# Hybrid attention layer on one core: q and k transposed in full by head pairs and split behind the transpose, first column sums ahead of the root's turn, two modulations together

## The chip, the core and the metric

One core of a Trainium2 chip runs the whole layer as one program. Its engines are TensorE (PE, with PEld for the weight loads that overlap its matmuls), VectorE (DVE), ScalarE (ACT), GpSimd (POOL) and SyncE (SP, which here issues most DMAs). The metric is the device time of one execution in microseconds.

## The reference

In outline. One decoder layer on a sequence of 512 tokens of width 1024. x is normalised by its root mean square and modulated by a scale and a shift computed from c; the result h goes through one wide projection to q, k, v and gates of two groups of eight heads of width 64, two key heads each.

```python
mod = silu(c) @ w_ada + b_ada
shift, scale, gate = split(mod, 3)
h = rms_norm(x, norm_gain) * (1 + scale) + shift
(q_a, k_a, v_a, z_a, q_b, kc, vc, ks, vs, kw, vw, z_b, g_b) = split(h @ w_in)
qa = qk_norm(q_a) * qscale;  ka = qk_norm(k_a)          # group A: window 128, sinks
o_a = banded_gqa(qa, ka, v_a, 128, rel_bias_a, sinks)
qb = qk_norm(q_b) * qscale                               # group B: three branches
k_cmp = qk_norm(compress(kc)); k_sel = qk_norm(ks); k_win = qk_norm(kw)
o_b = g0 * compressed(qb) + g1 * selected(qb) + g2 * window_512(qb)
y = concat(o_a * silu(z_a), o_b * silu(z_b))
out = x + gate * (y @ w_out)
```

With 8 blocks of 64 keys and a top-k of 16 the selected branch takes all blocks, so it is causal attention too.

## The kernel before

The sequence lies in four blocks of 128 tokens (NB = 4), the width in eight tiles of 128 (k = 0 to 7). A product that must keep f32 accuracy is made of three products in the faster type fp32r: each operand is split into a high part (a copy rounded to fp32r, on ACT) and a low part (the difference, on DVE), and high x high, high x low and low x high are summed in PSUM.

**First projection** (lines 300 to 438, in a strict written order on every engine, `in_order`). The squares of x are summed by matmuls, `rsqrt` is made on DVE from four columns, and `rbp` is its transposed broadcast, four PE transposes (L369), "the root's turn". For each width tile k the modulation needs two vectors: `mod_pe(k)` makes partial sums on PE (L228, evicted by ACT at L232 to `macc`), or `mod_dve(k)` makes them on DVE; `mod_col(k)` sums them over the partitions by PE (L259); `mod_ab(k)` (L264, L265) makes scale and shift from them, and `h_high` and `h_low` the two parts of h. `first_proj(k, n)` is PE's work for tile k and product n. `MOD_AFTER` says after which (k, n) which `mod_pe` stands, `COL_AFTER` the same for `mod_col`. Weights come through rings of NR = 4 slots, which SP's loads refill when a slot is read.

**The rest** is a list of slots, run four deep in a software pipeline (`run`): scores of a slot (L892) with their maximum on DVE (L897), exponentials on ACT, scaling, transposes of the probabilities (L940, L950, evicted by ACT at L941, L951), products with v (L967). Between the parts of a slot a `Stream` of other work, a generator, is advanced by a number of microseconds: every `yield` names the cost of the PE work just issued. The stream holds the other projections (`unit_nat` L484, `unit_col` L494, with weights split at L170 on ACT and L171 on DVE) and, one step of a "post" to one step of a unit, the preparation of q, k, gates and compressed keys. Outside the blocks of PE work that are ordered by hand, the tile framework plans the order of instructions on each engine at build.

**q and k.** `q_scale` is called for a pair of heads, four times for group A and four for group B; `k_scale` once for each of three key sets. Both normalise on DVE (`qn` L532, `kn` L555 and L557), split into high and low parts in `qc` or `kc` (ACT L535 or L559, DVE L536 or L560), and transpose the parts on PE with an fp32r identity (L541, L565) into two PSUM banks one after the other, four transposes each. For q a bank holds one head, high part in partitions 0 to 63 and low part in 64 to 127, evicted in one piece with reversed order in each block (`qs`, ACT L549 or DVE L547). For k a bank holds the high (then the low) parts of both key heads, and each is evicted twice, into both halves of the partitions (`kT`, ACT L569, DVE L570). `PT` gives out the two PSUM banks of all transposes in turn. The scores multiply 128 rows of `qs` (high and low) with `kT[:, 0]` (high twice) and `kT[:, 1]` (low twice).

The **last projection** (L494 with `yh`, `yl`) makes eight output tiles, each evicted by DVE with gate and residual (L1048) and stored.

Of the kernel before, what the change touches and what calls it, by code (L numbers as in the profile page):

```python
# [9 lines left out]
F32 = mybir.dt.float32  # L10
F32R = mybir.dt.float32r
I32 = mybir.dt.int32
BF16 = mybir.dt.bfloat16
AF = mybir.ActivationFunctionType
OP = mybir.AluOpType
# [4 lines left out]
S, D, HD, NB = 512, 1024, 64, 4  # L20
# [5 lines left out]
LINE = 640  # L26
GW = 280
AHEAD = 6
NT2 = 38
WAIT_L, WAIT_M = 4, (0, 8)  # L30
PER_A, PER_B = 3.6, (3.5, 1.6, 7)
ND = (16, 3, 4)
NR = 4
LW = 4
MOD_AFTER = {(0, 0): (1,), (1, 0): (2,), (2, 0): (3,), (3, 2): (5,)}
COL_AFTER = {(0, 1): (1,), (1, 1): (2,), (2, 1): (3,), (3, 1): (4,), (4, 0): (5,), (5, 0): (6,), (6, 1): (7,)}


def rev(ap):

    dims = [list(e) for e in ap.ap]
    step, n = dims[-1]
    dims[-1] = [-step, n]
    return bass.AP(tensor=ap.tensor, offset=ap.offset + step * (n - 1), ap=dims)
# [37 lines left out]
def hybrid_layer_kernel(ctx, tc, A, out):  # L82
    nc = tc.nc
    PE, DVE, ACT, POOL, SP = nc.tensor, nc.vector, nc.scalar, nc.gpsimd, nc.sync
# [3 lines left out]
    con = ctx.enter_context(tc.tile_pool(name="con", bufs=1))  # L88
    t2 = ctx.enter_context(tc.tile_pool(name="t2", bufs=NT2))
    rawp = ctx.enter_context(tc.tile_pool(name="rawp", bufs=5))  # L90
# [3 lines left out]
    def T2(dt, name):  # L94
        return t2.tile([128, S], dt, name=name, tag="t2")
# [17 lines left out]
    cT, prm, ident = first[:, 0:8], first[:, 8:40], first[:, 40:168]  # L113
# [4 lines left out]
    cmask = rest[:, 832:960].rearrange("p (a b) -> p a b", a=NB)  # L118
    qga, kga, qgb, kgs, kgw, kgc = (sml[:, 64 * i:64 * i + 64] for i in range(6))
    bnsa, sinks = sml[:, 384:408], sml[:, 408:416]  # L120
    ident_r = con.tile([128, 128], F32R, name="ident_r")
    ones = con.tile([128, 1], F32, name="ones")
    DVE.memset(ones, 1.0)

# [98 lines left out]
    def mod_pe(k):  # L223

        pm = ps_pj.tile([128, 512], F32, name="pj")[:, 0:256]
        for j in range(8):
            c = j % 4
            PE.matmul(pm[32 * c:32 * c + 32, :], scz[:, j, :], ada[k][:, j].rearrange("p a b -> p (a b)"),  # L228
                      start=j < 4, stop=j >= 4, skip_group_check=True)
        macc[k] = stp.tile([128, 2, 128], F32, name="macc0", bufs=2)  # L230
        yield
        ACT.activation(macc[k].rearrange("p a b -> p (a b)"), pm, AF.Copy)  # L232
# [22 lines left out]
    def mod_col(k):  # L255

        pc = pcs[k] = ps_pj.tile([128, 512], F32, name="pj")
        for s in range(2):
            PE.matmul(pc[:, s:s + 1], macc[k][:, s, :], ones, start=True, stop=True)  # L259
# [8 lines left out]
    def weights_high(k):  # L268

        ws[k] = (stp.tile([128, 768], F32R, name="swh", bufs=3), stp.tile([128, 768], F32R, name="swl", bufs=3))  # L270
        ACT.activation(ws[k][0], wst[k], AF.Copy)
# [4 lines left out]
    def scaled(k, by, parts=(slice(0, S),)):  # L276
        y[k] = xT[k]
        for c in parts:
            DVE.tensor_tensor(y[k][:, c], xT[k][:, c], by[:, c], op=OP.mult)
# [19 lines left out]
    with in_order(tc) as begun:  # L299
# [20 lines left out]
        def dummies(n):  # L320
            for _ in range(n):
                PE.matmul(pj_kv[0].rearrange("p a b -> p (a b)"), zero[:, 0:128], zero, start=True, stop=True)
# [3 lines left out]
        halves = [slice(0, 256), slice(256, 512)]  # L326
# [29 lines left out]
                              stop=k == 7 and tb == NB - 1, skip_group_check=True)  # L356
        for b in lines[2:]:
            next(b, None)
        ACT.activation(ident_r, ident, AF.Copy)
        for a in range(2):  # L360
            SP.dma_start(line_d[a], lsb[a])
        sx = con.tile([128, NB], F32, name="sx")
# [1 line left out]
        rx = rsqrt(sx, NB)  # L364
        for _ in mod_pe(0):
            pass
        rbp = ps_pj.tile([128, 512], F32, name="pj")
        for tb in range(NB):
            PE.transpose(rbp[:, tb * 128:(tb + 1) * 128], rx[:, tb:tb + 1].to_broadcast([128, 128]), ident)  # L369
        mod_col(0)  # L370
        dummies(ND[2])
        weights_high(0)
        scaled(0, rbp, halves[:1])
        mod_ab(0)
        scaled(0, rbp, halves[1:])
        rb = stp.tile([128, S], F32, name="rb")
        hf[0] = T2(F32, "hf")
        for c in halves:
# [36 lines left out]
        for k in range(8):  # L415
# [6 lines left out]
            for n in range(3):  # L422
                first_proj(k, n)
                for m in MOD_AFTER.get((k, n), ()):
                    for _ in mod_pe(m):
# [14 lines left out]
    mp = ctx.enter_context(tc.tile_pool(name="mp", bufs=1))  # L440

    def W2(name, shape=(128, 512)):
        return mp.tile(list(shape), F32, name=name, tag="w2", bufs=5)
# [22 lines left out]
    def PT():  # L466
        return ps_t.tile([128, 512], F32, name="pt")
# [36 lines left out]
        chain.update(last)  # L504


    qs = {}
    kT = {}
    kTb = {}
# [18 lines left out]

    def q_scale(src, rn, heads):

        qn = W2("qn", (128, 8, HD))
        DVE.tensor_tensor(qn.rearrange("p (t h) d -> p t h d", t=NB), src,  # L532
                          rn[:, :, :, None].to_broadcast([128, NB, 2, HD]), op=OP.mult)
        qc = mp.tile([128, 8, 2, HD], F32R, name="qc", tag="qc", bufs=2)
        ACT.activation(qc[:, :, 0, :], qn, AF.Copy)  # L535
        DVE.tensor_tensor(qc[:, :, 1, :], qn, qc[:, :, 0, :].bitcast(F32), op=OP.subtract)  # L536
        yield 0.0
        for n, h in enumerate(heads):
            pt = PT()
            for tb in range(NB):  # L540
                PE.transpose(pt[:, tb * 128:(tb + 1) * 128].bitcast(F32R),  # L541
                             qc[:, 2 * tb + n].rearrange("p a d -> p (a d)"), ident_r)
            qs[h] = T2(F32R, f"qs{h}")
            dst = qs[h].rearrange("p (t q) -> p t q", t=NB)
            src_ = rev(pt.rearrange("p (t q) -> p t q", t=NB))
            if n:
                DVE.tensor_copy(dst, src_)  # L547
            else:
                ACT.activation(dst, src_, AF.Copy)  # L549
            yield 0.44  # L550

    def k_scale(ty, src, rn):

        kn = W2("kn", (128, 8, HD))
        DVE.tensor_tensor(kn, src.rearrange("p t (g d) -> p (t g) d", d=HD), rn[:, :, None].to_broadcast([128, 8, HD]),  # L555
                          op=OP.mult)
        DVE.tensor_tensor(kn, kn, kg[:, ty:ty + 1, :].to_broadcast([128, 8, HD]), op=OP.mult)  # L557
        kc = mp.tile([128, 2, 8, HD], F32R, name="kc", tag="qc", bufs=2)
        ACT.activation(kc[:, 0], kn, AF.Copy)  # L559
        DVE.tensor_tensor(kc[:, 1], kn, kc[:, 0].bitcast(F32), op=OP.subtract)  # L560
        yield 0.0
        for hl_ in range(2):
            pt = PT()
            for t in range(NB):
                PE.transpose(pt[:, t * 128:(t + 1) * 128].bitcast(F32R),  # L565
                             kc[:, hl_, 2 * t:2 * t + 2].rearrange("p g d -> p (g d)"), ident_r)
            for g in range(2):
                src_ = pt[64 * g:64 * g + 64, :]
                ACT.activation(kT[ty, g][0:64, hl_, :], src_, AF.Copy)  # L569
                DVE.tensor_copy(kT[ty, g][64:128, hl_, :], src_)  # L570
            yield 0.44

    rn_a = {}

# [545 lines left out]
```

## Time and profile before

| | |
|---|---|
| median of 3 runs | 325.29 us (324.1 to 432.5) |
| profiled execution, its own time | 324.27 us |
| its span from the first to the last instruction | 322.2 us |
| PE, PEld, DVE, ACT busy | 97%, 80%, 73%, 61% |
| granted TensorE clock | 0.999 of full |

Busy time of PE includes the latency of matmuls that overlap, so a busy PE isn't PE at its peak. Times in the trace are counted from the first instruction of the span. PE is the same engine as PEld; a wait can show on either of the two queues or on both.

### The profile page before, as it was taken

To read this page: it belongs to the slowest core of one execution; us is meant where nothing else is said; L and a number is where in the kernel's file an instruction comes from. 1 tells how busy PE (TensorE), PEld (TensorE's weight loads), DVE (VectorE), ACT (ScalarE), POOL (GpSimd) and SP (SyncE) were. 2 spreads that over 40 slices of the span, in tenths; PEclk is the share of its full clock that TensorE was granted. 3 is DMA by queue.
4 is the path that set the end of the run, shared out by engine and by line. 5 is a ranking of instruction groups with operands and counts; after the bars stand their busy time and mean duration, and the time that the engine had idled before them with its cause. 6 is when DMAs were issued, how large, how long until landed. Compare 5 with 4: busy or idle time off the path is not lost.

```text
span 322.2 us, 6131 instructions
## 1 busy us (share of the span) xinstructions
PE 312.7 (97%) x2232; PEld 259.0 (80%) x2232; DVE 235.6 (73%) x691; ACT 196.2 (61%) x477; POOL 4.9 (2%) x22
## 2 busy tenths in 40 slices
PE   7899999999999999999999999999999999999995
PEld 2577888888999888989977787788788788788883
DVE  3658597999888268878899789899779788544320
ACT  4565545965986474986958658787587575502200
POOL 1000000000010000000000000000000000000000
PEclk9999999999999999999999999999999999999999
DMA  8999975800065248130042270045422134034301
GB/s 238 394 409 409 400 240 133 301 3 3 0 189 172 67 137 290 34 113 21 33 130 41 94 197 0 2 125 203 131 67 70 63 110 152 33 101 166 125 33 65
DMA packets 31061, 44.26 MB, mean 137 GB/s; under 512 B 1767, under 2 KB 23399, under 8 KB 31033
## 3 DMA queue, kind: packets, MB, share of 16 engines
q1 hardware_dynamic: 29880, 41.79, 38.8%
q10 hardware_dynamic: 1152, 2.10, 2.4%
q8 instruction: 17, 0.28, 0.3%
q14 instruction: 12, 0.09, 0.1%
HBM read 41.74 MB, written 2.14 MB: 136 GB/s over the span
## 4 chain that ended last, share of the span: by engine, by line
PE 73%; DVE 14%; DMA 6%; ACT 4%; issue 2%; SPq 1%; DVEq 0%; ACTq 0%
PE pj L494 23%; PE pj L484 9%; PE sq L295 7%; PE s L892 6%; PE po L967 6%; PE skv L296 4%; PE pt L940 3%; DMA raw<-in_w_z_b 3%; PE pt L950 3%; DVE wl L171 3%; DVE pp L897 2%; PE s L620 2%; PE pj L228 2%; DMA raw<-in_bias 1%; DMA raw<-in_w_q_b 1%
## 5 line engine op out<-in xcount | busy, mean ns | idle before, releaser
L170 ACT ACTIVATE wh<-raw 128x512 fp32r<-128x512 f32 (+1 forms) x52 | 31.2, 635 | 25.0 <-PE pj L494 14.6
L171 DVE TENSOR_TENSOR wl<-raw,wh 128x512 fp32r<-128x512 f32 (+1 forms) x52 | 35.2, 691 | 8.1 <-ACT wh L170 4.6
L484 PE MATMUL pj<-wh,hh 128*128 128x256 f32 (+1 forms) x128 | 36.8, 289 | 0.4 <-ACT wh L170 0.4
L484 PE MATMUL pj<-wh,hl 128*128 128x256 f32 (+1 forms) x128 | 36.9, 288 | 0.0
L484 PE MATMUL pj<-wl,hh 128*128 128x256 f32 (+1 forms) x128 | 36.4, 286 | 0.0
L904 ACT ACTIVATE pp<-pp,nm 128x256 f32<-128x256 f32 (+2 forms) x48 | 29.3, 612 | 5.9 <-DVE nm L897 5.4
L494 PE MATMUL pj<-hh,wh 128*128 128x512 f32 x80 | 32.6, 407 | 0.0
L494 PE MATMUL pj<-hh,wl 128*128 128x512 f32 x80 | 32.1, 402 | 0.0
L494 PE MATMUL pj<-hl,wh 128*128 128x512 f32 x80 | 31.9, 399 | 0.0
L897 DVE CUSTOM_DVE_ANT_0 pp<-s,bias 128x256 f32<-128x256 f32 (+2 forms) x48 | 25.6, 548 | 4.6 <-PE s L892 4.6
L494 PE MATMUL pj<-yh,wl 128*128 128x512 f32 x64 | 25.5, 398 | 0.0
L494 PE MATMUL pj<-yh,wh 128*128 128x512 f32 x64 | 25.4, 399 | 0.0
L494 PE MATMUL pj<-yl,wh 128*128 128x512 f32 x64 | 25.3, 395 | 0.0
L484 PEld LDWEIGHTS pj<-wh,hh 128*128 128x128 f32 x128 | 24.0, 188 | 0.6 <-ACT wh L170 0.6
L484 PEld LDWEIGHTS pj<-wl,hh 128*128 128x128 f32 x128 | 24.1, 189 | 0.2 <-issue 0.2
L484 PEld LDWEIGHTS pj<-wh,hl 128*128 128x128 f32 x128 | 24.1, 188 | 0.1
L892 PE MATMUL s<-kTb,qs 128*128 128x256 f32 (+2 forms) x96 | 23.4, 357 | 0.0
L897 DVE CUSTOM_DVE_ANT_0 pa<-s,bias,nsink 128x256 f32<-128x256 f32 (+1 forms) x32 | 14.3, 448 | 10.5 <-PE s L892 9.1
L951 ACT COPY ptT<-pt 128x384 f32<-128x384 f32 (+1 forms) x32 | 16.0, 527 | 9.3 <-PE pt L950 8.5
L925 DVE TENSOR_SCALAR pp<-pp,rr,grev 128x256 f32<-128x256 f32 (+2 forms) x48 | 21.4, 473 | 0.3
L1048 DVE SCALAR_TENSOR_TENSOR fin<-pj,gate,xr 128x512 f32<-128x512 f32 x8 | 6.0, 751 | 20.1 <-PE pj L494 20.1
L941 ACT COPY ptT<-pt 128x512 f32<-128x512 f32 (+1 forms) x28 | 15.4, 549 | 7.7 <-PE pt L940 7.4
(240 smaller groups left out, 727.6 us busy)
## 6 DMA issues: line engine op xcount, KB each, us to landing
ada_ring<-in_w_ada_ss SPq DMA_DIRECT2D x16, 512.0 KB, 7.3
raw<-in_w_cmp SPq DMA_DIRECT2D x8, 512.0 KB, 7.6
raw<-in_w_gate SPq DMA_DIRECT2D x8, 512.0 KB, 4.7
raw<-in_w_o SPq DMA_DIRECT2D x8, 512.0 KB, 3.8
wst_ring<-in_w_qkv_a SPq DMA_DIRECT2D x8, 384.0 KB, 9.3
xTp<-in_xT SPq DMA_DIRECT2D x8, 256.0 KB, 4.5
bias<-line_d SPq DMA_DIRECT2D x8, 256.0 KB, 3.8
raw<-in_w_q_b SPq DMA_DIRECT2D x4, 512.0 KB, 4.3
```

What stands on the lines that cost most here:

```text
L170: ACT.activation(wh, src, AF.Copy)
L171: DVE.tensor_tensor(wl, src, wh.bitcast(F32), op=OP.subtract)
L295: PE.matmul(pj_q[tb], lt, w[:, 0:512], start=f, stop=l, skip_group_check=True)
L484: PE.matmul(bank[:, t * n:(t + 1) * n], h[:, tb * 128:(tb + 1) * 128], w[:, k % 2, :], start=k == 0 and m == 0, stop=k == 7 and m == 2)
L494: PE.matmul(bank, w, h, start=k == 0 and m == 0, stop=k == 7 and m == 2)
L892: PE.matmul(ps, qs[h][:, 128 * i:128 * i + 128], k[:, hl_, lo:lo + w], start=hl_ == 0, stop=hl_ == 1)
L897: DVE.tensor_tensor_reduce(out=P[:, g, 0:w], in0=ps, in1=bt, scale=1.0, scalar=init, op0=OP.add, op1=OP.min, accum_out=nm[:, g:g + 1])
L904: ACT.activation(P[:, g, 0:e], P[:, g, 0:e], AF.Exp, bias=nm[:, g:g + 1], scale=-1.0, accum_out=dn[:, g:g + 1])
L925: DVE.tensor_scalar(v, v, rr[:, g:g + 1], gates[:, g, br:br + 1], op0=OP.mult, op1=OP.mult)
L941: ACT.copy(T[:, :, 0:nb, :], rev(pt[:, 0:2 * nb * 128].rearrange("p (g b q) -> p g b q", g=2, b=nb)))
L951: ACT.copy(T[:, 0:nb, :], rev(pt[:, 0:nb * 128].rearrange("p (b q) -> p b q", b=nb)))
L967: PE.matmul(o[64 * g:64 * g + 64, 128 * i:128 * i + 128], vb[:, 64 * g:64 * g + 64], sl["T"][g][:, b, :], start=first_of and b == 0, stop= ...
```

## The change

Four edits. (1) `q_scale` and `k_scale` transpose the normalised f32 values of a pair of heads at once, four transposes into one bank with the f32 identity, and make the two parts while evicting: ACT writes the rounded high part, DVE subtracts it from the same half of the bank. For the second head of a pair the high part lies in partitions 64 to 127 and the low one in 0 to 63. The tiles `qc`, `kc` and the fp32r identity `ident_r` go, each generator has one `yield 0.44` less, and the ring of general tiles has 40 slots instead of 38 (`NT2`). (2) `mod_col(0)` stands ahead of the four transposes of the root instead of behind them. (3) `mod_ab(0)` stands ahead of both halves of `scaled(0)` on DVE instead of between them. (4) `mod_pe(3)` stands right behind `mod_pe(2)`, after product 0 of tile 1, instead of after product 0 of tile 2.

```diff
-NT2 = 38
+NT2 = 40
...
-MOD_AFTER = {(0, 0): (1,), (1, 0): (2,), (2, 0): (3,), (3, 2): (5,)}
+MOD_AFTER = {(0, 0): (1,), (1, 0): (2, 3), (3, 2): (5,)}
...
-    ident_r = con.tile([128, 128], F32R, name="ident_r")
...
-        ACT.activation(ident_r, ident, AF.Copy)
...
         for _ in mod_pe(0):
             pass
+        mod_col(0)
         rbp = ps_pj.tile([128, 512], F32, name="pj")
         for tb in range(NB):
             PE.transpose(rbp[:, tb * 128:(tb + 1) * 128], rx[:, tb:tb + 1].to_broadcast([128, 128]), ident)
-        mod_col(0)
         dummies(ND[2])
         weights_high(0)
-        scaled(0, rbp, halves[:1])
         mod_ab(0)
-        scaled(0, rbp, halves[1:])
+        scaled(0, rbp, halves)
...
+    HALF = (slice(0, 64), slice(64, 128))
...
     def q_scale(src, rn, heads):
         qn = W2("qn", (128, 8, HD))
         DVE.tensor_tensor(qn.rearrange("p (t h) d -> p t h d", t=NB), src,
                           rn[:, :, :, None].to_broadcast([128, NB, 2, HD]), op=OP.mult)
-        qc = mp.tile([128, 8, 2, HD], F32R, name="qc", tag="qc", bufs=2)
-        ACT.activation(qc[:, :, 0, :], qn, AF.Copy)
-        DVE.tensor_tensor(qc[:, :, 1, :], qn, qc[:, :, 0, :].bitcast(F32), op=OP.subtract)
         yield 0.0
+        pt = PT()
+        for tb in range(NB):
+            PE.transpose(pt[:, tb * 128:(tb + 1) * 128], qn[:, 2 * tb:2 * tb + 2].rearrange("p a d -> p (a d)"), ident)
+        blocks = lambda ap: ap.rearrange("p (t q) -> p t q", t=NB)
         for n, h in enumerate(heads):
-            pt = PT()
-            for tb in range(NB):
-                PE.transpose(pt[:, tb * 128:(tb + 1) * 128].bitcast(F32R),
-                             qc[:, 2 * tb + n].rearrange("p a d -> p (a d)"), ident_r)
             qs[h] = T2(F32R, f"qs{h}")
-            dst = qs[h].rearrange("p (t q) -> p t q", t=NB)
-            src_ = rev(pt.rearrange("p (t q) -> p t q", t=NB))
-            if n:
-                DVE.tensor_copy(dst, src_)
-            else:
-                ACT.activation(dst, src_, AF.Copy)
-            yield 0.44
+            high, low, part = blocks(qs[h][HALF[n], :]), blocks(qs[h][HALF[1 - n], :]), rev(blocks(pt[HALF[n], :]))
+            ACT.activation(high, part, AF.Copy)
+            DVE.tensor_tensor(low, part, high.bitcast(F32), op=OP.subtract)
+        yield 0.44
...
     def k_scale(ty, src, rn):
...
-        kc = mp.tile([128, 2, 8, HD], F32R, name="kc", tag="qc", bufs=2)
-        ACT.activation(kc[:, 0], kn, AF.Copy)
-        DVE.tensor_tensor(kc[:, 1], kn, kc[:, 0].bitcast(F32), op=OP.subtract)
         yield 0.0
-        for hl_ in range(2):
-            pt = PT()
-            for t in range(NB):
-                PE.transpose(pt[:, t * 128:(t + 1) * 128].bitcast(F32R),
-                             kc[:, hl_, 2 * t:2 * t + 2].rearrange("p g d -> p (g d)"), ident_r)
-            for g in range(2):
-                src_ = pt[64 * g:64 * g + 64, :]
-                ACT.activation(kT[ty, g][0:64, hl_, :], src_, AF.Copy)
-                DVE.tensor_copy(kT[ty, g][64:128, hl_, :], src_)
-            yield 0.44
+        pt = PT()
+        for t in range(NB):
+            PE.transpose(pt[:, t * 128:(t + 1) * 128], kn[:, 2 * t:2 * t + 2].rearrange("p g d -> p (g d)"), ident)
+        for g in range(2):
+            part, k = pt[HALF[g], :], kT[ty, g]
+            for e in (g, 1 - g):
+                ACT.activation(k[HALF[e], 0, :], part, AF.Copy)
+            for e in (g, 1 - g):
+                DVE.tensor_tensor(k[HALF[e], 1, :], part, k[HALF[g], 0, :].bitcast(F32), op=OP.subtract)
+        yield 0.44
```

## Rows read from the trace of the kernel before

**Rows 1.** The page's first part: busy time of each engine in us, its share of the span, and its number of instructions.

```profile
PE 312.7 (97%) x2232; PEld 259.0 (80%) x2232; DVE 235.6 (73%) x691; ACT 196.2 (61%) x477; POOL 4.9 (2%) x22
```

**Rows 2.** The table of stretches: the stretch and its length in us, busy time and instructions of PE, PEld, DVE, ACT and POOL, the granted clock as a share of full speed, the DMA engines' busy share and GB/s. Here are the first projection, the three stretches in which q and k are prepared, and the last projection.

```profile
17.20:59.30 42.10, 42.10 (x285) 34.42 (x286) 31.36 (x73) 23.74 (x41) 0.00 (x0) 1.00 0.88 316
59.30:95.00 35.70, 34.72 (x244) 31.03 (x243) 32.94 (x87) 28.04 (x72) 1.67 (x7) 1.00 0.21 67
95.00:146.00 51.00, 50.02 (x443) 45.85 (x442) 35.02 (x123) 35.26 (x99) 1.82 (x9) 1.00 0.44 144
146.00:176.00 30.00, 29.84 (x227) 26.33 (x225) 26.33 (x83) 22.71 (x57) 0.00 (x0) 1.00 0.19 54
...
277.80:322.20 44.40, 40.75 (x175) 32.72 (x175) 16.57 (x25) 7.86 (x14) 0.00 (x0) 0.99 0.29 95
```

**Rows 3.** The chain of work that ended last, in order of time: start, length, and what it was. This is its longest piece, near the end.

```profile
277.79 40.78 PE pj L494 x175
```

**Rows 4.** The waits between 60 and 176 us: engine and line, what was waited for, us in total, how often, the longest.

```profile
PEld pt L541 <- DVE qc L536: 1.4, 3, 0.7
...
PEld pt L565 <- ACT kc L559: 0.6, 2, 0.4
...
PE pt L541 <- DVE qc L536: 0.6, 1, 0.6
```

**Rows 5.** Of the tile `pt`, the PSUM banks of the transposes: the transposes of q and k, with count, shortest, median and longest duration in ns, and the start of the first and the last in us.

```profile
L541 PE MATMUL pt<-ident_r,qc x64: 222/248/283, 72.3 to 172.3; 128*128 128x128 f32 x64
...
L565 PE MATMUL pt<-ident_r,kc x24: 221/248/282, 67.9 to 133.3; 128*128 128x128 f32 x24
```

**Rows 6.** PE's instructions in order of time around one group of four fp32r transposes of q: start, length of the run of equal instructions, and the instruction with its count.

```profile
72.22 0.28 PE L484 MATMUL pj<-wh,hl 128*128 128x256 f32 x1
72.34 0.46 PE L541 MATMUL pt<-ident_r,qc 128*128 128x128 f32 x4
72.63 0.35 PE L484 MATMUL pj<-wh,hh 128*128 128x256 f32 x1
72.82 0.28 PE L484 MATMUL pj<-wl,hh 128*128 128x256 f32 x1
```

**Rows 7.** The same around one group of four f32 transposes with the f32 identity (it lies in the tile `first`).

```profile
179.08 0.60 PE L950 MATMUL pt<-first,pp 128*128 128x128 f32 x4
179.44 0.48 PE L494 MATMUL pj<-hh,wh 128*128 128x512 f32 x1
179.75 0.40 PE L494 MATMUL pj<-hl,wh 128*128 128x512 f32 x1
```

**Rows 8.** The groups of instructions by line with different shapes apart: line, engine, operation, output and inputs, shapes (partitions x elements), count, busy us, mean ns of one, and the idle time before them with what ended it. They are the split and the evictions of q and k, two DVE operations of one size with and without a PSUM operand, and ACT's eviction of the slots' transposes.

```profile
L941 ACT COPY ptT<-pt 128x512 f32<-128x512 f32 x24 | 13.9, 580 | 4.9 <-PE pt L940 4.6
...
L547 DVE CAST qs<-pt 128x512 fp32r<-128x512 f32 x8 | 5.5, 687 | 0.3 <-PE pt L541 0.2
...
L570 DVE CAST kTb<-pt 64x512 fp32r<-64x512 f32 x8 | 5.4, 689 | 0.9 <-ACT kTb L569 0.8
L536 DVE TENSOR_TENSOR qc<-qn,qc 128x512 fp32r<-128x512 f32 x8 | 5.4, 690 | 0.3
L535 ACT ACTIVATE qc<-qn 128x512 fp32r<-128x512 f32 x8 | 5.0, 627 | 5.1 <-DVE qn L532 5.1
...
L549 ACT ACTIVATE qs<-pt 128x512 fp32r<-128x512 f32 x8 | 4.8, 594 | 3.6 <-PE pt L541 3.5
...
L279 DVE TENSOR_TENSOR xTp<-xTp,pj 128x256 f32<-128x256 f32 x2 | 0.8, 418 | 0.8 <-PE pj L369 0.8
...
L340 DVE TENSOR_TENSOR sacc<-sacc,sq 128x256 f32<-128x256 f32 x2 | 0.8, 420 | 0.1
```

**Rows 9.** In order of time, one call of `k_scale` near 100 us: start, length, instruction; in brackets the idle time of its engine just before it and what ended it.

```profile
98.70 0.69 DVE L557 TENSOR_TENSOR kn<-kn,kg 128x512 f32<-128x512 f32 x1
...
100.10 0.69 DVE L560 TENSOR_TENSOR kc<-kn,kc 128x512 fp32r<-128x512 f32 x1 [0.60 <-ACT kc L559]
...
100.69 2.67 ACT L569 ACTIVATE kTb<-pt 64x512 fp32r<-64x512 f32 x4 [0.47 <-PE pt L565]
...
101.32 2.77 DVE L570 CAST kTb<-pt 64x512 fp32r<-64x512 f32 x4 [0.53 <-ACT kTb L569]
```

**Rows 10.** In order of time, the end of the start: from the first modulation's eviction to the first part of h.

```profile
14.46 0.38 ACT L232 ACTIVATE macc<-pj 128x256 f32<-128x256 f32 x1 [2.23 <-PE pj L228]
...
15.21 0.62 PE L369 MATMUL pj<-first,n_y 128*128 128x128 f32 x4 [0.81 <-PE pj L228]
...
15.67 0.50 PE L259 MATMUL pj<-ones,macc 128*128 128x1 f32 x4
15.87 0.42 DVE L279 TENSOR_TENSOR xTp<-xTp,pj 128x256 f32<-128x256 f32 x1 [0.76 <-PE pj L369]
...
16.28 0.21 DVE L265 SCALAR_TENSOR_TENSOR AB<-pj,prm,first 128x1 f32<-128x1 f32 x1
...
16.53 1.09 ACT L379 ACTIVATE hh<-xTp,AB 128x256 fp32r<-128x256 f32 x2 [0.95 <-DVE AB L265]
```

**Rows 11.** In order of time, the second modulation's matmuls on PE: start, length, instruction and count.

```profile
24.62 1.07 PE L228 MATMUL pj<-ada_ring,scz 128*32 128x256 f32 x16
```

**Rows 12.** In order of time, SP's two loads of the weights of the third modulation: start, time from the start of the first to the end of the second, instruction and count.

```profile
13.73 1.30 SPq L200 DMA_DIRECT2D ada_ring<-in_w_ada_ss  x2
```

**Rows 13.** Of the tile `ada_ring`, all loads of the ring together: the shortest, median and longest time from issue to landing in us.

```profile
DMA to landing us min/median/max: 5.8/7.3/10.3
```

## The prediction

> **What bounds the kernel now.** I read the page's busy shares first: TensorE (PE) is busy in 97% of the span, VectorE (DVE) in 73% and ScalarE (ACT) in 61% [rows 1]. A share over the whole span hides the stages, so the table of stretches came next. In the first projection (17.2 to 59.3 us) PE has no idle time at all. In the three stretches in which q and k are prepared it is busy 34.72 of 35.7 us, 50.02 of 51.0 and 29.84 of 30.0, and in the last projection it runs without a break to its last matmul [rows 2]: the chain of waits ends in 175 matmuls of 40.78 us, 0.233 us each [rows 3]. So whatever PE work is taken out shortens the time, unless another engine then sets the pace. The candidate is DVE: 32.94 of 35.7 us busy between 59.3 and 95 us, 26.33 of 30.0 between 146 and 176, but only 35.02 of 51.0 between [rows 2]. Last I looked at what PE waited for at the edited lines: the weight loads of the q transposes waited 1.4 us in all for the difference made on DVE, one matmul of theirs 0.6 us (the same 0.7 us stop near 74.7 us seen on both queues), and the k transposes 0.6 us for ACT's rounded copy [rows 4]. The granted clock is 1.00 in each of these stretches but the last, where it is 0.99 [rows 2], so it is no part of the sum.
>
> **The transposes.** Eight calls of q_scale and three of k_scale make 64 + 24 = 88 transposes of fp32r data [rows 5]: eight per call, in two groups of four. After the change each call makes one group of four on plain f32, 44 in all. A group of four fp32r ones, inserted between other matmuls: it starts at 72.34 where the next L484 matmul would have, and the second L484 after it starts at 72.82; less one L484 pitch (72.34 - 72.22 = 0.12) that is 0.36 us [rows 6]. The f32 form is in the trace too, with the same identity: four of them start at 179.08, and the second L494 after them at 179.75; 0.67 less one pitch of 0.233 is 0.44 us [rows 3, 7]. Per call 2 x 0.36 - 0.44 = 0.28 us, and for 11 calls **-3.1 us** of PE work. All 11 calls lie between 67 and 173 us [rows 5], where PE is at or above 97% [rows 2].
>
> The Trainium skill (FP8 and Floating Point Precision, TensorE Precision Notes) says that true FP32 takes four passes through the array. By that an f32 transpose of 128 columns would be an estimated 0.21 us, a group 0.85 us, and the change would cost 11 x 0.13 = 1.4 us. This trace doesn't agree: four f32 transposes go in at 0.44 us a group, so this has no chance of its own here.
>
> **What stands before the transposes.** Before, qn passes through an ACT copy (0.627 us) and a DVE difference (0.690) and only then to PE [rows 8]; after, PE takes qn at once. The waits of rows 4 (1.4 + 0.6 = 2.0 us on the load queue; the 0.6 on the matmul is the same time again) are for those two steps and go. But the next late thing at the same places is qn or kn itself, and in the queue ahead of the transposes stands work that DVE still owes. I take 0.8 us of the 2.0, that is little more than the one large stop: **-0.8 us**, bounds 0 and -2.0.
>
> **What stands behind them.** For q: before, ACT and DVE evicted a bank each, side by side (0.594 and 0.687 [rows 8]). After, for each head ACT copies the high half and DVE subtracts it from the same PSUM half: ACT 2 x 0.6, DVE 2 x 0.69, the first difference behind the first copy. An operation on 64 partitions costs what one on 128 costs (0.689 for the 64x512 cast [rows 8]), and a DVE tensor_tensor with one operand in PSUM costs the same as with none (0.418 against 0.420 for 128x256 [rows 8]), so DVE's and ACT's sums for q stay: three DVE operations and two ACT ones a call, as before. From qn to the last half it was 0.63 + 0.69 + 0.36 + 0.69 = 2.4 with the second group's start hidden; it becomes 0.44 + 0.60 + 2 x 0.69 = 2.4 us. So the scores that need q come no earlier and no later: 0.
>
> For k: the ACT copy and the DVE difference go, the four ACT and four DVE evictions stay: 3 x 0.63 less on ACT, 3 x 0.69 less on DVE. In the trace DVE's first cast starts at 101.32, after ACT's first copy, begun at 100.69, has ended, while ACT goes on with the other half; DVE idled 0.53 us for it [rows 9]. In the new order ACT reads each half twice before DVE does, so I let the first difference wait for two copies: 0.44 + 1.2 + 4 x 0.69 = 4.4 us from kn, against 99.4 to 104.1, 4.7 us, in the trace [rows 9]. Again about 0. The DVE time saved is worth something only where DVE is full, in the k call of the first stretch: 0 to -0.7, I take 0, since the splits of weights stand in the same queue.
>
> The Trainium skill (PSUM — Partial Sum Buffer, PSUM bank collisions raise a hardware error) holds that two engines may not even read one bank in the same quarter of its partitions at once, which speaks against a shared half: by it the k difference waits 1.2 instead of 0.6 us, and if each of the six halves showed on PE's path the sum would be 3.6 us worse. The trace agrees with the order (0.53 us of idle above), not with a place on PE's path, which stays busy there.
>
> The new waits: each difference on DVE waits for ACT's copy of its half, and behind it in DVE's queue stand the splits of weights (L171) and the maxima of the scores (L897), which feed PE. A PSUM bank of the transposes (two exist) is held longer, 0.44 + 0.6 + 2 x 0.69 = 2.4 us for q instead of two for about 1.0 each (0.36 and one eviction); before, though, one call took both banks. Cost 0 in the sum, upper bound in the rival below.
>
> **The start.** The column sums L259 move ahead of the root's transposes. They wait for ACT's copy, done at 14.84, and take at most 0.50 us together; the transposes start about 15.38 instead of 15.21, and DVE's first half at 16.04 instead of 15.87. In exchange the pair L264, L265 no longer stands between that half and ACT: hh starts at 16.04 + 0.42 + 0.04 = 16.50 instead of 16.53 [rows 10]. Nothing, between -0.2 (transposes not delayed) and +0.4 us (the sums late, everything behind them). ACT's ident_r copy goes from ahead of 2.23 us in which ACT idles [rows 10]: 0. The third modulation moves from tile 2 to tile 1: its matmuls take 1.07 us in either place [rows 11], PE is full before and after [rows 2]. Its weights were issued by 14.70 and take 10.3 us at most to land: 25.0, against a new start near 25.7 [rows 11 to 13]. It is moved past SP's later loads only in freeing its ring slot some 5 us earlier. 0, and +0.6 if it lands late. NT2 of 40 removes no wait that the trace shows: 0.
>
> **The sum** is made against the profiled execution, 324.27 us (span 322.2): -3.1 - 0.8 = -3.9, so **320.4 us**. The median of the three runs is 325.29, 1.0 above that execution; 2%, 6.5 us, is about what a measurement of this kernel can tell from no change, and 3.9 lies within it.
>
> **The rivals.** (A) More waits go: all 2.0 us ahead of the transposes, 0.7 from DVE in the first stretch, 0.2 at the start: -3.1 - 2.9 = -6.0, 318.3 us. For it: DVE at 92% from 59.3 to 95 us. Against: these waits have successors close behind.
>
> (B) DVE takes the gain: in the calls of 59.3 to 95 and 146 to 176 us what PE saves comes back as waits for DVE, whose work for q is not less. Then only the k calls near 100 and 131 us count: -0.6 - 0.8 = -1.4, 322.9 us. For it: DVE's shares of 92% and 88%; against it: PE was the fuller engine in both.
>
> (C) Slower: the bank. If each of the 11 calls holds the one bank that the slots' transposes need next, PE waits for it; the price is an eviction of 0.58 us (L941 [rows 8]) a call, 6.4 in all: -3.1 + 6.4 = +3.3, 327.6 us. It decides from 0.28 us a call on, where the transposes' gain is used up. Against it: the second bank is now free in each call.
>
> That the change doesn't do what it says would be the f32 transposes at another price; rows 7 show that price. One thing no row prices: outside the start the order on DVE and ACT is planned at build, and the stream now asks 11 x 0.44 = 4.8 us less of its turn, so its units move ahead of the slots. I allow 1.5 us either way.
>
> **How the numbers follow.** Forecast 0.50, (A) 0.15, (B) 0.25, (C) 0.10. The range from 317.0 to 325.3 reaches past (A) and (B) with the 1.5 us of the order and leaves out (C) and the far ends. Faster by over 2% means under 318.8: most of (A) and the lower tail of the forecast, 0.17; slower by over 2% needs more than (C), 0.04; the rest 0.79.
>
> **What would show it.** 44 f32 transposes at these lines, about 0.11 us apart, with no load waiting for a difference; PE's busy time 3 us less and the idle time between 59.3 and 176 us not more than before. (B) would show as PE waiting for L897 or L171 after 146 us; (C) as weight loads of L940 or L950 waiting for the new difference. It is wrong if the planned order shifts a whole slot, or if the difference with its PSUM operand takes longer than 0.69 us.

## The result and the profile after

The changed kernel takes **322.86 us** (median of 20 runs, 322.06 to 326.03), the kernel before 324.75 us beside it (20 runs): a ratio of 0.995, 95% interval 0.9933 to 0.9967. That is 1.6 us off the median of before shown above by the ratio, 1.9 us by the medians of the same session; 3.9 us were forecast. The profiled execution of after took 322.34 us (span 320.6) against 324.27 (322.2). The sign is right and the time lies in the range, but half of the gain is missing.

The page's first part for after, which answers to [rows 1]:

```profile
PE 311.4 (97%) x2187; PEld 256.1 (80%) x2188; DVE 234.9 (73%) x688; ACT 195.8 (61%) x473; POOL 4.5 (1%) x22
```

PE has 45 matmuls fewer, the 44 transposes that went (a few records can be missing), and is busy 1.3 us less where 3 were expected. The table of stretches of after, with the columns of [rows 2]:

```profile
17.20:59.30 42.10, 41.78 (x285) 33.99 (x284) 31.50 (x72) 23.93 (x41) 0.00 (x0) 1.00 0.97 347
59.30:95.00 35.70, 34.64 (x231) 30.67 (x231) 33.96 (x92) 28.85 (x74) 1.70 (x9) 1.00 0.22 61
95.00:146.00 51.00, 50.41 (x443) 46.20 (x441) 35.80 (x127) 34.32 (x95) 1.41 (x7) 1.00 0.41 130
146.00:176.00 30.00, 29.73 (x208) 23.55 (x206) 22.75 (x70) 21.43 (x51) 0.00 (x0) 1.00 0.14 45
```

From 146 to 176 us PE is as busy as before, 29.73 of 30.0 us, and the clock is 1.00, so no loss shows. But busy time holds the latency of matmuls that overlap (the f32 transposes below last 0.27 us each and start 0.11 us apart), and equal stretches don't hold equal work: after runs a block of small matmuls inside this stretch that before runs right behind it, from 175.99 us on. That block is looked into below. The tile of the transposes, as in [rows 5] (shortest, median, longest ns, and where):

```profile
L536 PE MATMUL pt<-first,qn x32: 270/273/329, 68.2 to 167.5; 128*128 128x128 f32 x32
...
L554 PE MATMUL pt<-first,kn x12: 272/273/328, 67.7 to 131.5; 128*128 128x128 f32 x12
```

The 44 f32 transposes are there. One group of four between the projection's matmuls, as in [rows 6]:

```profile
77.98 0.60 PE L536 MATMUL pt<-first,qn 128*128 128x128 f32 x4
78.34 0.37 PE L481 MATMUL pj<-wh,hh 128*128 128x256 f32 x1
78.54 0.28 PE L481 MATMUL pj<-wl,hh 128*128 128x256 f32 x1
```

78.54 - 77.98 less one pitch of 0.12 is 0.44 us, the price forecast. The waits of after between 60 and 176 us, as in [rows 4], those of the new lines:

```profile
ACT qs L541 <- DVE qs L542: 4.6, 5, 1.3
...
DVE qs L542 <- ACT qs L541: 2.2, 5, 0.8
...
ACT kT L558 <- DVE kT L560: 1.2, 1, 1.2
...
PEld pt L536 <- DVE qn L531: 0.8, 2, 0.6
...
PEld pt L554 <- DVE kn L550: 0.6, 2, 0.3
...
PE pt L930 <- DVE pa L919: 0.6, 1, 0.6
PEld s L882 <- ACT qs L541: 0.6, 1, 0.6
```

The waits of the transposes for a difference are gone; 0.8 and 0.6 us of waits for `qn` and `kn` stand in their place. New is that ACT waits for DVE's difference (4.6 us) before it copies the other head from the same bank, and that scores on PE wait for a head: 0.6 us in one place, near 75 us, where before has no such wait.

To compare kernels without what happens at the start, I take from each trace the first and last matmul of the first projection and the last matmul of all. Before: 17.18, 59.04 and 318.16 us; after: 17.81, 59.46 and 316.55. So the start lost 0.63, the first projection gained 0.2 (41.66 instead of 41.86), and **the rest**, from the end of the first projection on, gained 2.04 (257.08 instead of 259.12). "Rest" means this span below; each is read from one execution. Two executions of one kernel gave 257.08 and 257.29 (after and e9), and 257.25 and 257.23 (e5 and e10), so differences of 0.2 us say nothing.

### The profile page after: what moved, and what is told of

Its sections match the earlier page's. It is cut to its first block, busy times and chain, and to the rows that moved or that the text cites. A ratio compares the mean times of both kernels' runs of the same rounds, so it can differ in the third digit from the quotient of the medians.

```text
span 320.6 us, 5999 instructions
## 1 busy us (share of the span) xinstructions
PE 311.4 (97%) x2187; PEld 256.1 (80%) x2188; DVE 234.9 (73%) x688; ACT 195.8 (61%) x473; POOL 4.5 (1%) x22
## 4 chain that ended last, share of the span: by engine, by line
PE 84%; DVE 6%; ACT 5%; DMA 2%; issue 1%; SPq 1%; POOL 0%; ACTq 0%; POOLq 0%
PE pj L491 30%; PE pj L481 9%; PE sq L294 8%; PE po L957 8%; PE s L882 7%; PE pt L940 4%; PE skv L295 4%; PE pt L930 3%; PE s L610 2%; DMA raw<-in_bias 2%; PE pj L227 2%; PE po L963 1%; DVE qs L542 1%; ACT pa L894 1%; PE pj L258 1%
## 5 line engine op out<-in xcount | busy, mean ns | idle before, releaser
L491 PEld LDWEIGHTS pj<-hh,wh 128*128 128x128 f32 x80 | 15.1, 188 | 4.7 <-issue 2.0
```

Of the source, the lines that this page charges most:

```text
L491: PE.matmul(bank, w, h, start=k == 0 and m == 0, stop=k == 7 and m == 2)
```

## Where the missing gain is: a torn block

Group B's compressed branch multiplies `qs` with `kTc` in 16 small matmuls (L678, L668 after the change), eight heads into two banks, two matmuls for each head in the trace. They run in the stream right behind the last call of `q_scale`. PE in order of time, before:

```profile
171.73 0.81 PE L541 MATMUL pt<-ident_r,qc 128*128 128x128 f32 x8
...
175.99 1.07 PE L678 MATMUL s<-qs,kTc 128*32 128x512 f32 x8
176.87 1.04 PE L678 MATMUL pj<-qs,kTc 128*32 128x512 f32 x8
177.85 0.50 PE L494 MATMUL pj<-hh,wh 128*128 128x512 f32 x1
```

and after:

```profile
167.09 0.66 PE L536 MATMUL pt<-first,qn 128*128 128x128 f32 x4
...
168.26 1.06 PE L668 MATMUL s<-qs,kTc 128*32 128x512 f32 x6
169.25 0.50 PE L491 MATMUL pj<-hh,wh 128*128 128x512 f32 x1
...
170.37 0.62 PE L668 MATMUL s<-qs,kTc 128*32 128x512 f32 x1
170.37 0.63 PE L668 MATMUL pj<-qs,kTc 128*32 128x512 f32 x3
170.82 0.59 PE L668 MATMUL s<-qs,kTc 128*32 128x512 f32 x1
170.83 0.61 PE L668 MATMUL pj<-qs,kTc 128*32 128x512 f32 x3
171.36 0.49 PE L491 MATMUL pj<-hl,wh 128*128 128x512 f32 x1
...
172.02 1.05 PE L668 MATMUL pj<-qs,kTc 128*32 128x512 f32 x2
173.00 0.66 PE L930 MATMUL pt<-first,pp 128*128 128x128 f32 x4
```

Before, 16 in one piece take 177.85 - 175.99 = 1.86 us (1.85 from unrounded starts). After, pieces of 6, 8 and 2 take 0.99, 1.00 and 0.98: 2.96 us, 1.1 more. A piece of two costs as much as one of eight.

The starts in the trace show why. These matmuls use 32 columns each (`128*32`), and up to four heads start within 0.02 us of each other; their second matmuls follow in the same way 0.43 to 0.45 us later, as at 170.37 and 170.82. So a piece takes two such rounds whether it holds one head or four: six rounds after, four before, which is 2 x 0.43 = 0.86 us more. From a piece's last round to the next matmul of 128 columns it is 0.52 to 0.54 us, so a piece costs about 0.13 us besides its rounds, twice more after than before. Together that is the 1.1 us. The Trainium skill (TensorEngine Tiling (Array Packing), Key Properties) says that a change of tiling mode drains the engine. At most the 2 x 0.13 us can be that here.

Why it is torn can be read on ACT and DVE. After, the last call's transposes start at 167.09, and its two heads are made so:

```profile
167.66 0.60 ACT L894 ACTIVATE pp<-pp,nm 128x384 f32<-128x384 f32 x1
...
168.26 0.58 ACT L541 ACTIVATE qs<-pt 64x512 fp32r<-64x512 f32 x1
...
168.59 0.48 DVE L915 TENSOR_SCALAR pp<-pp,rr,grev 128x384 f32<-128x384 f32 x1
169.10 0.68 DVE L542 TENSOR_TENSOR qs<-pt,qs 64x512 fp32r<-64x512 f32 x1
...
169.88 0.59 ACT L541 ACTIVATE qs<-pt 64x512 fp32r<-64x512 f32 x1 [1.04 <-DVE qs L542]
...
170.51 0.69 DVE L542 TENSOR_TENSOR qs<-pt,qs 64x512 fp32r<-64x512 f32 x1 [0.21 <-ACT qs L541]
```

The last half is done at 171.20, 4.1 us behind the transposes; the last two small matmuls come at 172.02. Before, the last call's eight transposes start at 171.73, and

```profile
172.23 0.60 ACT L549 ACTIVATE qs<-pt 128x512 fp32r<-128x512 f32 x1 [0.43 <-PE pt L541]
172.96 0.68 DVE L547 CAST qs<-pt 128x512 fp32r<-128x512 f32 x1
```

end it at 173.64, 1.9 us behind them, with 2.35 us to spare before the block at 175.99. So two things came together: the heads are ready later behind their transposes, and with one pause fewer per call the block comes sooner. That the planner put other matmuls into the block because the heads were late is my reading (in e11 and e13, where the block comes later, it is whole, which agrees); that the tear costs 1.1 us was tried (e13).

## The experiments

**e1, e2: the two halves of the change.** e1 is the change of q and k alone (with the 40 slots), e2 the start and the modulation alone.

> Only the first edit (q and k transposed in full, 40 slots); the start and the modulations as before. Theory of the turns: the one PSUM bank of a call makes ACT and DVE take strict turns, and all of the 1.9 us gained and of the 2 us missing lie in this part: 322.9 us, ratio 0.995. Theory of the start: the other edits cost 0.4 to 0.6 us instead of nothing (the first product of the first projection began at 17.81 instead of 17.18 us): 322.3 us, ratio 0.993, and its first projection begins at 17.2 us again.

> Only the other edits: first column sums ahead of the root's turn, scale and shift ahead of both halves, two modulations together; q and k as before. Theory of the turns: no change beyond noise, ratio 1.000, first projection begins at 17.2 us when the bias rows land as early as before. Theory of the start: 0.4 to 0.6 us slower, ratio 1.0015 to 1.002.

Measured: e1 323.1 us, ratio 0.995 (0.9934 to 0.9965), rest 257.12; e2 324.0 us, 0.9989 (0.9972 to 1.0005), rest 259.04, first projection 41.56. The whole effect is that of q and k; the start and the modulation can't be told from nothing.

**e3: one hand-over a call.** ACT copies both halves first, DVE makes both differences then; for k likewise.

```diff
-            ACT.activation(high, part, AF.Copy)
-            DVE.tensor_tensor(low, part, high.bitcast(F32), op=OP.subtract)
+            ACT.activation(high, part, AF.Copy)
+            halves_.append((low, part, high))
+        for low, part, high in halves_:
+            DVE.tensor_tensor(low, part, high.bitcast(F32), op=OP.subtract)
```

> The changed kernel, but each call makes all its copies on ACT first and then all its differences on DVE: one hand-over of the bank between the engines instead of three. Theory of the turns: ACT no longer waits for DVE at the copies (4.6 us in the changed kernel, then 0), and 0.5 to 1.0 us come back: 321.9 to 322.4 us, ratio to the kernel before 0.991 to 0.993. Rival, the size: the transposes save less than 0.28 us a call and the turns cost nothing: 322.9 us as the changed kernel.

Measured: 323.07 us, 0.9953 (0.9934 to 0.9972), rest 256.94. ACT's waits for DVE are gone from the view of waits, the time is that of the changed kernel. The block of the compressed branch is in one piece here, but PE stops inside it, and it still takes 2.68 us.

**e4, e7, e8: more transposes.** e4 makes the four transposes twice, into two banks, and reads each head from a bank of its own; e7 makes them twice into the one bank; e8 makes each of the old fp32r groups twice.

```diff
-        pt = PT()
-        for tb in range(NB):
-            PE.transpose(pt[...], ...)
+        pts = [PT(), PT()]
+        for pt in pts:
+            for tb in range(NB):
+                PE.transpose(pt[...], ...)
```

> The changed kernel, but each call makes its four f32 transposes twice, into two PSUM banks, and reads one head from each: no turns, 44 transposes more. If PE sets the pace at these places they cost 11 x 0.44 = 4.8 us: 327.7 us when the turns cost nothing; theory of the turns: 1 to 2 us less than that, 325.7 to 326.7 us. If DVE sets the pace instead, the added transposes are hidden: 323 to 324 us.

> The changed kernel with each group of four f32 transposes made twice into the same bank: 44 more. By the prediction's price of 0.44 us a group 4.8 us more, 327.7 us. Theory of the size, that a group costs PE more at these places than between other matmuls: 5.5 to 6.5 us more, 328.4 to 329.4 us, as with two banks.

> The kernel before with each group of four fp32r transposes made twice into the same bank: 88 more. By the prediction's price of 0.36 us a group 7.9 us more, 332.6 us. Theory of the size, that the fp32r groups cost less than that: 6.0 to 7.0 us more, 330.7 to 331.7 us, so that 22 of them less 11 f32 groups are worth 0.5 to 1 us instead of 3.1.

Measured: e4 329.06 us, 1.0151 (1.0121 to 1.018), rest 263.02; e7 330.17, 1.0189 (1.0155 to 1.0223), rest 262.91 (its profiled execution, 331.39 us, began the first projection only at 20.38 us); e8 332.28, 1.025 (1.0221 to 1.0278), rest 266.56. With a bank for each head the waits between 59 and 180 us are

```profile
DVE kTb L562 <- ACT kTb L560: 2.6, 2, 1.4
DVE qs L543 <- ACT qs L542: 1.6, 2, 0.8
```

and none of ACT for DVE. So the turns come from the shared bank. The Trainium skill (PSUM — Partial Sum Buffer, PSUM bank collisions raise a hardware error) has two engines collide on a bank only in the same quarter of its partitions. In the changed kernel ACT waits 4.6 us although it copies the other half, so the program as built keeps the two apart by the whole bank. But e4 and e7 have the same rest within 0.1 us, so no cost of the turns as such shows on PE; as the order differs between the two as well, that is a sign and no proof. The added groups cost their full price: (262.91 - 257.08) / 11 = 0.53 us for an f32 group, (266.56 - 259.12) / 22 = 0.34 for an fp32r one. By these the transposes' term would be 22 x 0.34 - 11 x 0.53 = 1.6 us, not 3.1. I took that for the answer until e11: these kernels also move the order of everything behind, which is worth as much as the difference.

**e5, e6, e9, e10: the residual's tiles.** In the kernel before, the tiles `xr` of the last projection shared the ring of `qc`, and so waited for the last `qc`. Without `qc` their first two loads are issued at the very start. The DMA issues of the first 10 us of after:

```profile
xTp<-in_xT SPq DMA_DIRECT2D x8, 256.0 KB, 4.6
...
xr<-in_xT ACTq DMA_DIRECT2D x2, 256.0 KB, 3.4
```

e5 and e10 put `xr` into a ring that is in use until later; e6 is the kernel before with a ring of its own for `xr`, so that these loads are early there too; e9 is the changed kernel again.

```diff
-        xr = mp.tile([128, S], F32, name="xr", tag="qc", bufs=2)
+        xr = mp.tile([128, S], F32, name="xr", tag="bias", bufs=4)
```

> The changed kernel, but the residual tiles xr of the last projection share the ring of the bias tiles, as they shared that of qc before: their first two loads (2 x 256 KB on ACT's queue) can't be issued at the very start any more. Theory of the early loads: they delay the loads of x, so the first projection begins at 17.1 to 17.3 us instead of 17.7 to 18.2, and the time is 0.5 to 0.8 us less than the changed kernel: 322.0 to 322.4 us, ratio to the kernel before 0.992 to 0.993. Rival, chance in the landing of the loads: 322.9 us, ratio 0.995, with the start as late as in the changed kernel.

> The kernel before, with one edit: xr has a ring of its own, so its first two loads may be issued at once. Theory of the early loads: 0.5 to 0.8 us slower than the kernel before, 325.1 to 325.4 us, ratio 1.0015 to 1.0025, first projection from 17.7 us on. Rival: ratio 1.000.

> The changed kernel once more, on the same chip and against the same runs of the kernel before as the next three, so that differences of half a microsecond can be read. Both theories expect 0.995 of the kernel before.

> The changed kernel with the residual's tiles in a ring that is still in use early, so that their loads can't be issued at the start. Theory (the early loads cost the start 0.5 to 0.7 us): 0.5 to 0.7 us less than the changed kernel of this call, a ratio of 0.993 to 0.9935, and the first product of the first projection at about 17.1 us instead of 17.7. Rival (the start gains, but the time is lost again before the end): the same time as the changed kernel within 0.2 us.

Measured: e5 322.6 us, 0.9958 (0.9937 to 0.9979); e6 324.93, 1.0022 (1.0007 to 1.0037); e9 322.96, 0.9953 (0.993 to 0.9976); e10 322.52, 0.9949 (0.9923 to 0.9975). In the kernel before the early loads cost 0.2 to 1.2 us (e6). In the changed one the sign agrees between e9 and e10 (0.44 us, first product at 17.51 and 17.23), but the intervals overlap, and the ratio of e5 is no better than that of the changed kernel (0.995). The first product of kernels that are the same up to there came at 16.68 (e14) to 18.03 (e12). So 0.63 us at the start of one execution proves nothing by itself.

**e11: both pauses.** e10 with the second pause of each call put back; no work is changed.

```diff
         yield 0.44
+        yield 0.44
```

> The run before with the second pause of 0.44 us back in each call for q and k, so that the stream asks as much of its turn as in the kernel before, and its units don't move ahead of the slots. Theory (the shorter stream costs or gives nothing that matters): the same as the run before within 0.3 us. Rival (the units that move ahead are why waits of the slots' transposes for their scaling grew from 1.3 to 3.0 us): about 1 us less than the run before, with the waits ahead of the slots' transposes down by as much.

Measured: **320.28 us**, 0.9876 (0.9849 to 0.9902), rest 255.35, 2.2 us better than e10 beside it. The last link of the chain of waits, after and e11:

```profile
278.09 38.87 PE pj L491 x167
```

```profile
274.10 40.79 PE pj L491 x175
```

Against 277.79 and 175 matmuls in [rows 3], the slots of e11 end 3.69 us earlier with the same work left. Those of after end 0.30 later, with eight matmuls fewer left. The block of the compressed branch takes 1.85 us in e11. The rival was right that time is won, but not in why: counted by the starts of PE's matmuls, the stops ahead of the slots' transposes between 60 and 176 us fell only from 2.4 us in e10 to 2.1.

**e12: less for ACT and DVE in k.** e10, but ACT and DVE make each part of k once, and GpSimd copies both parts to the other half of the partitions.

> The run two before with half of the evictions of k taken from ScalarE and VectorE: they make each part of k once, and GpSimd copies both parts to the other half of the partitions in SBUF. In the three calls for k VectorE then makes two differences of about 0.69 us instead of four, so it is about 4 us less busy in all. Theory (VectorE doesn't set the time, TensorE's own work does): the same as the run two before within 0.3 us, or slower where the copies come late. Rival (VectorE takes part of the gain, in its turns with ScalarE on one bank): 0.7 us or more less.

Measured: 322.18 us, 0.993 (0.9905 to 0.9955), rest 257.67 against 257.23 in e10. Six of twelve differences and as many copies of k gone from DVE and ACT gain nothing: they aren't the pace.

**e13: the block alone.** e10 with two empty steps ahead of the compressed branch's scores; up to there nothing differs.

```diff
     def cmp_attn():
+        for _ in range(2):
+            yield 0.0
```

> The changed kernel with the late residual tiles, and two empty pauses (of no time) ahead of the scores of the compressed branch, so that these come two steps of the stream later; up to there nothing differs. In the program as built their 16 matmuls then stand in one piece. Theory 1 (the torn block): it takes 1.85 us instead of 2.97, and the kernel 1.1 us less than the changed one, some 321.4. Theory 2 (the stream asks too little time): nothing is gained, 322.5.

Measured: 321.44 us, 0.9909 (0.988 to 0.9938), rest 256.06, which is 1.17 less than e10. PE at the block:

```profile
171.69 1.06 PE L670 MATMUL s<-qs,kTc 128*32 128x512 f32 x8
172.57 1.04 PE L670 MATMUL pj<-qs,kTc 128*32 128x512 f32 x8
173.54 0.88 PE L942 MATMUL pt<-first,pp 128*128 128x128 f32 x6
```

One piece, 1.85 us. What the block gained (1.1) is what the rest gained, to 0.1 us, and the time is the one that theory 1 gave.

**e14, e15, e16: how much time, or how many steps.** e14 is e10 with one pause of 0.88 us, e15 with two of 0.22, e16 the kernel before with one of its two pauses taken out.

> The changed kernel with the late residual tiles, and 0.88 us instead of 0.44 in the single pause of each call for q and k: the stream's time of the kernel before, with one step fewer. As built, the block of the compressed branch is torn in three here too. Theory 1: the block takes 2.9 us, and the time is that of the changed kernel, 322.5. Theory 2: the time is that with both pauses, 320.3.

> The changed kernel with the late residual tiles, and two pauses of 0.22 us instead of one of 0.44: the steps of the kernel before, with the shorter time. As built, the block is in one piece. Theory 1: it takes 1.85 us and the kernel 321.4 or less. Theory 2: 322.5.

> The kernel before with one of the two pauses of 0.44 us taken out of each call for q and k, as the change does, and nothing else changed. As built, the block of the compressed branch stays in one piece here. Theory 1: no loss, 324.4 as before within 0.5 us. Theory 2: about 2 us slower than the kernel before, 326.3.

Measured: e14 323.53 us, 0.9967 (0.9951 to 0.9983), rest 259.25, block 3.94 in four pieces; e15 323.8, 0.9976 (0.9956 to 0.9995), rest 258.32, block 1.99; e16 326.42, 1.0054 (1.0033 to 1.0074), rest 260.79, block 1.86. Neither theory holds as a rule. The block is whole or torn as theory 1 said (though in four pieces in e14, not three), but its times are missed in all three; e15 loses elsewhere what it wins there. One place is the start of the last projection:

```profile
281.23 0.97 PE L491 MATMUL pj<-yh,wh 128*128 128x512 f32 x3 [1.06 <-ACT yh L820]
```

And e16 loses 1.7 us without any change of work and with its block whole; theory 2 had the size, but the equal time of e14 and e15 speaks against an amount of time as the cause. What is shown: with the same work the order alone moves the rest from 255.35 (e11) to 259.25 us (e14), by 3.9 us, as much as the gain that was forecast. Pairs with equal pauses agree on what the change is worth: after against e16, one pause a call each, has 3.71 us less of rest, and e11 against before, two each, 3.77 less. The order differs within each pair as well (the block of after is torn, that of e16 whole), so the close agreement may be partly chance. What stays open is which stops make up e16's 1.7 us, and the 0.7 us by which e11 beats e13.

## Why the prediction was wrong

**What failed** is the step "So the scores that need q come no earlier and no later: 0", and with it the step that puts the order at 0 with a spread, "I allow 1.5 us either way". The last heads come 4.1 us behind their transposes, not 2.4 (and 1.9 before); over the eight q calls it is 3.4 to 7.1 us, against 1.5 to 3.0 before. The operations have the length that was forecast (0.58 and 0.69). Of the 1.7 us in the last call 0.7 is the turn: I let the second copy start behind the first one, but it stands behind DVE's first difference. The other 1.0 is that ACT begins 0.7 us late, behind exponentials of a slot, and DVE 0.3 late, behind a scaling. I then looked for who waits on ACT and DVE and not at what comes next in the stream, the block that needs all eight heads at once. Its tear cost 1.1 us (e13).

The order cost as much as is missing: one pause fewer a call lost 1.7 us of rest in the kernel before (e16) and 1.9 in the changed one (e10 against e11), while with equal pauses the change gained 3.7 to 3.8. That the two losses are alike makes no fixed price of a pause: e14 and e15 don't follow it. The allowance of 1.5 us was of about the right size, but as a symmetrical spread it hid that one place could be looked up: the stream's next step behind each of the 11 calls.

**The transposes, -3.1.** The group prices were read rightly (0.44 again above). In all, the calls' insertions between other matmuls, counted from the starts of PE's matmuls (against the median pitch of each kind; another choice of it moves a sum by some 0.5 us), took 10.0 us before, 1.5 of it idle ahead of them, and 6.7 after, 0.7 idle: the transposes alone -2.5, the waits -0.8. In e11 it is 5.9, with 0.8 idle: -3.4 and -0.7. So the term is -2.5 to -3.4 by the place in which the groups fall, and -3.1 lies between; the 1.6 us from doubling (e7, e8) is lower, and I hold it to be disturbed by the order, which isn't shown.

**The waits ahead of them, -0.8:** right, -0.8 by this count and -0.6 by the view of waits (1.4 us instead of 2.0), and for the reason given: `qn` and `kn` are late next.

**The sum for after** then is -2.5 - 0.8 + 1.1 = -2.2 for the rest, where -2.04 was measured; first projection -0.2, start +0.63, together -1.6 to the last matmul. With the order of e11 the rest is 3.77 us shorter than before: the forecast of 3.9 describes that kernel.

**The start:** ACT's first modulation eviction and `hh` of after are

```profile
15.13 0.38 ACT L231 ACTIVATE macc<-pj 128x256 f32<-128x256 f32 x1 [2.39 <-PE pj L227]
...
17.15 1.09 ACT L376 ACTIVATE hh<-xTp,AB 128x256 fp32r<-128x256 f32 x2 [0.87 <-DVE xTp L278]
```

2.02 us apart against 2.07 in [rows 10]; -0.03 was forecast. The modulation's move cost nothing, as said (e2). Missed was that taking `qc` away frees the ring on which `xr` waited: 0.2 to 1.2 us in e6, about 0.4, not resolved, in the changed kernel.

**The k calls:** [rows 9] were misread. ACT and DVE overlapped there because they were in two banks, not in two halves of one. After, near 100 us, they take strict turns:

```profile
99.10 1.19 ACT L558 ACTIVATE kTb<-pt 64x512 fp32r<-64x512 f32 x2 [2.21 <-PE pt L554]
100.86 1.37 DVE L560 TENSOR_TENSOR kTb<-pt,kTb 64x512 fp32r<-64x512 f32 x2
102.33 1.20 ACT L558 ACTIVATE kTb<-pt 64x512 fp32r<-64x512 f32 x2 [0.69 <-DVE kTb L560]
103.56 1.40 DVE L560 TENSOR_TENSOR kTb<-pt,kTb 64x512 fp32r<-64x512 f32 x2 [0.80 <-ACT kTb L558]
```

From `kn` (98.10) to the end 104.96 that is 6.9 us, where 4.4 were forecast. It cost PE nothing that e3 or e12 could show.

**The rivals.** (A), more waits go, didn't happen. (B) has the right time (322.9) by luck, for a wrong reason: DVE isn't the pace (e3, e12), and added PE work shows in full (e4, e7, e8). (C), the bank held, didn't happen on the scale of 0.58 a call; the largest single wait of the slots' transposes on the queue of PE's matmuls was for their scaling instead, which stood behind a new difference on DVE:

```profile
82.64 0.41 PE L930 MATMUL pt<-first,pa 128*128 128x128 f32 x2 [0.61 <-DVE pa L919]
```

where DVE ran L542 from 81.50 to 82.19 and L919 only from 82.20. That is the queue effect that the prediction named and priced at 0; PE's stops at these transposes (L940, L930 after the change) grew from 1.0 to 2.5 us between 60 and 176 us, not all of them for this reason, while those at the scores and the projections of L484 fell by 1.6.

## What to carry to other kernels

Where a planner lays out the work by costs given by hand, a change of the work is also a change of the order, and here the order was worth as much as the change (3.9 us of spread with equal work): keep the pauses as they were when you measure an edit, and try the pauses by themselves afterwards. For every product that now comes later, look up the next step that needs it in the list of work, above all blocks of small matmuls that are cheap only while four of them run side by side. And when a tile goes, ask who shared its ring, since their loads may now be issued much earlier.

## What was not expected of the hardware

A torn block pays for each piece: two 32-column matmuls between 128-column ones took 0.98 us, eight of them 1.00, since up to four of them start together. In e12 a DVE scaling that began beside a GpSimd copy took three times as long as the same one alone:

```profile
103.09 1.03 POOL L560 CAST kTb<-kTb 64x1024 fp32r<-64x1024 f32 x1 [0.36 <-DVE kTb L558]
...
103.26 1.02 DVE L919 TENSOR_SCALAR pa<-pa,rr 128x256 f32<-128x256 f32 x1
...
106.76 0.35 DVE L919 TENSOR_SCALAR pa<-pa,rr 128x256 f32<-128x256 f32 x1
```

It ends at 104.28, behind the copy's end at 104.12. The Trainium skill (SBUF — State Buffer, Terms) has DVE and GpSimd share a pair of ports that one of them holds for a whole instruction; these rows agree. One other operation was held beside a copy, a DVE product for `qn` that took 0.96 instead of 0.69 us; differences that read PSUM kept their 0.69 us beside the copies.
